# Seven-product pairs of a hybrid layer's attention: one wide matmul for both parts of the input, in place of two

## Chip, cores and metric

The kernel runs on one core of one Trainium2 chip. The metric is the device time of one execution in microseconds; the time before is the median of three runs. Beside the times there is one profiled execution with a trace of every instruction, and all durations and positions come from it. The core's engines are TensorE (PE in the profile; its weight loads are PEld), VectorE (DVE), ScalarE (ACT), GpSimd (POOL) and SyncE (SP), which here issues the weight transfers.

## What is computed

One decoder layer in fp32, on 512 tokens of width 1024: a SwiGLU feed-forward, a mixer, and a second feed-forward, each with a norm before and after. The mixer has two branches from one input projection `u @ w_in`: dilated attention with 12 heads in 3 groups, and a gated recurrence. Cut to the part around the change:

```python
u = rms_norm(h, mix_norm_pre[l])
proj = u @ w_in[l]
q, k, v, xr, yr, gl = jnp.split(proj, splits, axis=-1)
...
for g, (window, dilation) in enumerate(DILATED_GROUPS):
    o_g, lse_g = dilated_group_attention(q[:, :, g], k[:, :, g], v[:, :, g], ...)
alpha = jax.nn.softmax(jnp.stack(lses, axis=0), axis=0)
attn = jnp.einsum('gbsh,gbshe->bshe', alpha, jnp.stack(outs, axis=0))
...
gates = jax.nn.sigmoid(gl).reshape(B, S, N_BRANCHES, D_MODEL)
merged = gates[:, :, 0] * attn_d + gates[:, :, 1] * rec_d
h = h + rms_norm(merged @ w_out[l], mix_norm_post[l])
```

## The kernel before

**Three matmuls for one.** An fp32 operand x is kept as two tiles of a reduced format: a high part xh (a rounding copy on ScalarE, L302) and a low part xl (x minus xh on VectorE, L303); `split` at L301 issues both. A product w x is then wh xh + wh xl + wl xh, three matmuls that add up in one PSUM bank. Weights come from HBM in the order of one fixed stream (`raw_of`, L234, issued on SyncE, four buffers) and are split the same way into tiles of 1024 (`w8`, four buffers) or 512 columns (`w4`, two).

**Seven products for eight.** For two neighbouring blocks of 128 output columns (a "pair": a query head and its key head, or two blocks of the gates), the 2x2 block product (halves of the depth, halves of the tokens) is done with seven products p1 to p7 in place of eight (a Strassen-like scheme). Each product is 4 blocks of the depth by 3 matmuls, 128 x 128 weights against 256 tokens, in `seventh` (L709 to L717: L715 is wh xh, L716 wh xl, L717 wl xh). `w_forms` (L671) makes the seven weight combinations of a pair: adds on VectorE (L678, L679, L680 and one more) and three splits of 1024 columns and one of 512. `forms_of` (L615) makes the seven combinations of the input once, in three steps (`early` with L654 to L656, `middle`, `late`).

**A pair** (`seven`, L748) runs p1, p2, p6, p5, p7, p4, p3 into three accumulators of 256 columns. Products that share an accumulator add up in it, so intermediate values are copied away on the way: four ScalarE copies of 128 x 256 to SBUF (L759), and four VectorE adds of a bank and a copy (L764) give the four quarters of the result. Banks come from two pools, five called `acc` and three called `aux`.

**The attention stage.** After the first feed-forward's last product, `Boundary.block` (L530) adds the residual and norms each of four token blocks, and `Boundary.turn` (L545) transposes it in two halves: four transposes into a bank, a ScalarE copy of 512 (L552, the high part), a VectorE subtract of 512 (L553, the low part), and a ScalarE copy to `facc` (L554). The high and low parts of the mixer's input, `um_t`, are two tiles of high and two of low values. Then:
- `values_first` (L1114) computes the first group's values, 512 columns of weights against 128 tokens (L1123 to L1125), and transposes the last two blocks between;
- `values_two` (L1136) computes the two other groups' values by seven products of 24 matmuls each (L1165 to L1167; 512 columns wide), its weights' combinations (`add`, L1151) made on the chip from four large transfers `vals<-in_w` and the stream;
- `qk(0)` (L1237) runs three pairs (queries and keys of head 0 in the three groups); then for each of four heads `attend` (L1258) computes scores, the softmax and the output, beside the next head's `qk`;
- eight gate blocks as four pairs with sigmoids (L1374), and the product with the attention's output weights.

**The order.** A tile scheduler places the instructions of all engines from the program's text and its priorities: weight loads and their combinations and splits are ahead by `AHEAD` = 100, what empties PSUM by `EVAC` = 200. Each engine then works through its list in that fixed order. Waits are semaphores that the scheduler sets where data or buffers require them.

Of the kernel before, what the change touches and what calls it, by code (L numbers as in the profile page):

```python
# [16 lines left out]
P = 128  # L17
# [166 lines left out]
def hybrid_layer(ctx: ExitStack, tc: tile.TileContext, xT: bass.AP, xN: bass.AP, wst: bass.AP,  # L184
# [337 lines left out]
    class Boundary:  # L522

        def __init__(self, f, grow, his, los, kept):
            self.f, self.grow, self.his, self.los, self.kept = f, grow, his, los, kept
            self.u = {}

        def block(self, b, sums):  # L530
# [14 lines left out]
        def turn(self, b):  # L545
            for i, u in enumerate(self.u.pop(b)):
                ps = aux_ps()
                for j in range(4):
                    PE.transpose(ps[:, j * P:(j + 1) * P], u[:, j * P:(j + 1) * P], ident)
                src = ps.rearrange("p (k t) -> p k t", k=4)  # L550
                hi, lo = (t[:, :, b * P:(b + 1) * P] for t in (self.his[i], self.los[i]))
                ACT.activation(hi, src, AF.Copy)  # L552
                DVE.tensor_sub(lo, src, hi.bitcast(F32))  # L553
# [13 lines left out]
    def x_forms(gname, r, pool):  # L567

        spool[0] = pool
        ha, hc = hs["t"]  # L570
        x00, x01, x10, x11 = ha[:, :, 0:HB], ha[:, :, HB:T], hc[:, :, 0:HB], hc[:, :, HB:T]
        t, d = {}, {}

        def form(name, src, tile_=None):
            v = tile_ if tile_ is not None else big([P, 2, 4, HB])
            t[name] = v[:, 0], v[:, 1]
# [35 lines left out]
    def tx_slot(pool, bufs=1):  # L612
        return pool.tile([P, 2, 4, HB], F32R, name="tx", tag="tx", bufs=bufs)

    def forms_of(x, his, los, pool, copied, rb=None):  # L615


        spool[0] = pool
        fx = facc.rearrange("p k t -> p (k t)").rearrange("p (b c) -> p b c", b=4)

        def quarter(i, j):
            return fx[:, 2 * j:2 * j + 2, i * T:i * T + T]

        two = []

        def slot():
            if not copied and not two:
                v = rb()
                two.extend(v[:, 4 * i:4 * i + 4, :].rearrange("p (s j) t -> p s j t", s=2) for i in range(2))
            if two:  # L630
                return two.pop(0)
            return tx_slot(pool).rearrange("p s k t -> p s (k t)").rearrange("p s (b c) -> p s b c", b=2)

        x01, x10, x11 = quarter(0, 1), quarter(1, 0), quarter(1, 1)
        t, d = {}, {}
        for name, i, j in (("p1", 0, 0), ("p2", 1, 0), ("p3", 1, 1)):
            t[name] = tuple(z[i][:, :, HALVES[j]] for z in (his, los))

        def copies():
            for name in ("p1", "p2", "p3"):  # L640
                v = big([P, 2, 4, HB])
                for i in range(2):
                    nc.gpsimd.dma_start(v[:, i], t[name][i])
                t[name] = v[:, 0], v[:, 1]

        def form(name, v, src):
            t[name] = tuple(v[:, i].rearrange("p b (k t) -> p k b t", k=4) for i in range(2))
            split(v[:, 0], v[:, 1], src)

        def early():  # L650
            if copied:
                copies()
            d[1], d[2] = (pool.tile([P, 2, T], F32, name="ts", tag="s", bufs=2) for _ in range(2))
            DVE.tensor_sub(d[1], quarter(0, 0), x01)  # L654
            DVE.scalar_tensor_tensor(d[2], x11, -1.0, d[1], op0=ALU.mult, op1=ALU.subtract)
            DVE.tensor_sub(x01, x11, x01)  # L656

        def middle():
            form("p6", slot(), d[2])
            DVE.scalar_tensor_tensor(d[2], d[2], -1.0, x10, op0=ALU.mult, op1=ALU.subtract)  # L660
            form("p5", big([P, 2, 2, T]), d[1])

        def late():
            form("p7", big([P, 2, 2, T]), x01)
            form("p4", big([P, 2, 2, T]) if copied else slot(), d[2])

        return t, [early, middle, late]
# [39 lines left out]
                    "p6": b[:, :, lo], "p3": b[:, :, hi], "p4": d}  # L707

    def seventh(t, w, p, ps, start):  # L709
        if len(t[p][0].shape) == 4:  # L710
            ps = ps.rearrange("q (b t) -> q b t", b=2)
        for k in range(4):
            ks = slice(k * P, (k + 1) * P)
            wh, wl, xh, xl = w[p][:, 0, ks], w[p][:, 1, ks], t[p][0][:, k], t[p][1][:, k]
            PE.matmul(ps, wh, xh, start=start and k == 0, stop=False, skip_group_check=True)  # L715
            PE.matmul(ps, wh, xl, start=False, stop=False, skip_group_check=True)  # L716
            PE.matmul(ps, wl, xh, start=False, stop=k == 3, skip_group_check=True)  # L717
# [27 lines left out]
        seventh(t, w, "p4", v, False)  # L745
        u0(v)

    def seven(t, w, z, g, u, seen=lambda ap: ap):  # L748


        b, y = acc_ps()[:, :HB], acc_ps()[:, :HB]
# [9 lines left out]

        def sum_of(dst, ps, c):
            with tc.high_priority(offset=EVAC):
                DVE.tensor_add(dst, seen(ps), seen(c))  # L764

        product("p1", b, True)
        c1 = copy(b)
# [305 lines left out]
    for b in range(4):  # L1073
        nc.gpsimd.dma_start(hb(b), xN[b])
    grow1, grow2 = gains(ap1, 0, 1)
    um_t = [big([P, 4, T]) for _ in range(4)]
    um = act_of(um_t[:2], um_t[2:])
    kept_m = dpool.tile([4, P, D], F32, name="kept_m")
    bd1 = Boundary(0.5, grow2, um_t[:2], um_t[2:], kept_m)

    def block1(b, sums):
        bd1.block(b, sums)
# [14 lines left out]
    with ExitStack() as mx:  # L1097
# [38 lines left out]
        def values_two(steps, then):  # L1136
# [23 lines left out]
            def prod(p, w, pss, start):  # L1160
                for j, ps in enumerate(pss):
                    for k in range(4):
                        xh, xl = (x[:, k, j * P:j * P + P] if len(x.shape) == 3 else x[:, k, j, :] for x in t[p])
                        wh, wl = (w[k // 2][:, i, k % 2 * T:k % 2 * T + T] for i in range(2))
                        PE.matmul(ps, xh, wh, start=start and k == 0, stop=False, skip_group_check=True)  # L1165
                        PE.matmul(ps, xh, wl, start=False, stop=False, skip_group_check=True)
                        PE.matmul(ps, xl, wh, start=False, stop=k == 3, skip_group_check=True)  # L1167
# [46 lines left out]
            prod("p4", w4_, v, False)  # L1214
            copies([vals[2][:, j, :] for j in range(2)], v, -1.0)

        t, steps = forms_of(um, um_t[:2], um_t[2:], apool, False, rec_half)
# [19 lines left out]
        def qk(hd):  # L1237

            q, k = [], []
            for g in range(NG):  # L1240
                w = pair_of(("pair",) + pairs[hd][g])
                tq, tk = (apool.tile([P, T], F32, name="qk", tag="qk", bufs=QKB) for _ in range(2))
                if g == 0:
                    seven(t, w, acc_ps()[:, :HB], *([nat(x)[:, 2 * i:2 * i + 2] for i in range(2)] for x in (tq, tk)),
                          seen=lambda ap: ap.rearrange("q (p b r) -> q p b r", p=2, b=4))
# [142 lines left out]
    with ExitStack() as mx:  # L1388
# [202 lines left out]
        for c in range(KC):  # L1591
            if c < 3:
                ps = pss[c]
            else:
# [14 lines left out]
    bd2 = Boundary(1.0, grow4, his, los, kept)  # L1609
# [6 lines left out]
    end2 = ffn(2, u2, None, forms_of(u2, his, los, ap2, True), ap2, pss)  # L1616
    new_h()
    for b in range(4):
        nc.gpsimd.dma_start(hb(b), kept[b])
# [139 lines left out]
```

## Time and profile before

| | |
|---|---|
| median of three runs | 1215.32 us (1214.71 to 1215.39) |
| profiled execution, first to last instruction | 1213.2 us |
| median less that span | 2.1 us |
| mean granted TensorE clock | 0.999 |
| TensorE's instructions | 7754 matmuls, 7754 weight loads |
| VectorE, ScalarE | 1536 and 1393 instructions |
| HBM read, written | 138.06 MB, 6.29 MB |
| stage around the change | values from 369 us, a head's period 39.5 us, gates after the last head |

How to read the rows shown below. In a row of a group stand the line, the engine, the operation, output and inputs by their names in the program, the shape (partitions x elements), the count after "x", then the busy time in us and the mean duration of one in ns, and last the idle time of the engine just before them with what ended it. A row of the timeline begins with the start in us and the duration. A row of waits reads: engine, tile and line that waited, what it waited for, then the time in us in all, how often, and the longest. TensorE's matmuls overlap in the pipe: a duration there is longer than the distance to the next start.

### The profile page before, as it was taken

How to read it: one execution, taken by the hardware profiler on the slowest of the kernel's cores; microseconds unless marked ns; L12 is line 12 of the kernel's file. 1: busy time of each engine (PE TensorE's matmuls, PEld its weight loads, DVE VectorE, ACT ScalarE, POOL GpSimd, SP SyncE). 2: the span in 40 equal slices, each digit the busy share in tenths (PEclk: the TensorE clock that was granted, in tenths of full speed). 3: DMA queues.
4: the chain of work that ended last, by engine and by line, in shares of the span. 5: the costliest groups of instructions: out<-in, count | busy, mean ns of one | idle time of the engine just before them, and what ended most of it. 6: DMA issues, size and time to landing. Idle time of an engine off the chain costs nothing.

```text
span 1213.2 us, 19767 instructions
## 1 busy us (share of the span) xinstructions
PE 1203.3 (99%) x7754; PEld 1099.5 (91%) x7754; DVE 1010.1 (83%) x1536; ACT 815.9 (67%) x1393; POOL 26.1 (2%) x51
## 2 busy tenths in 40 slices
PE   9999999999999999999999999999999999999997
PEld 8899999999888999999989888888899999999996
DVE  7999888989689888888767899875799888889964
ACT  6566787887566565566735898844566677878763
POOL 0000000000011000000000000000100000000000
PEclk9999999999999999999999999999999999999999
DMA  7233333334624232222213342235443333433341
GB/s 266 87 102 125 123 139 111 135 120 155 245 109 143 83 100 96 71 96 87 91 67 123 130 148 88 90 119 179 152 140 110 120 136 107 137 115 129 123 173 70
DMA packets 45822, 149.83 MB, mean 124 GB/s; under 512 B 5152, under 2 KB 8608, under 8 KB 45728
## 3 DMA queue, kind: packets, MB, share of 16 engines
q1 hardware_dynamic: 38160, 131.09, 31.9%
q0 software_dynamic: 7280, 17.30, 4.3%
q8 instruction: 61, 1.00, 0.3%
q14 instruction: 33, 0.27, 0.1%
q10 hardware_dynamic: 288, 0.17, 0.0%
HBM read 138.06 MB, written 6.29 MB: 119 GB/s over the span
## 4 chain that ended last, share of the span: by engine, by line
PE 91%; DVE 5%; DMA 2%; ACT 1%; issue 1%; DVEq 0%
PE acc L715 14%; PE acc L716 14%; PE acc L717 14%; PE acc L315 7%; PE acc L317 7%; PE acc L316 7%; PE aux L966 4%; PE aux L967 3%; PE aux L968 3%; DVE w L303 2%; PE acc L433 2%; PE acc L431 2%; PE acc L432 2%; DMA raw<-in_w 2%; PE aux L433 1%; PE aux L431 1%
## 5 line engine op out<-in xcount | busy, mean ns | idle before, releaser
L717 PE MATMUL acc<-big,w 128*128 128x256 f32 x1240 | 351.8, 284 | 0.0
L715 PE MATMUL acc<-big,w 128*128 128x256 f32 x1240 | 351.6, 284 | 0.0
L716 PE MATMUL acc<-big,w 128*128 128x256 f32 x1240 | 351.3, 283 | 0.0
L303 DVE TENSOR_TENSOR w<-raw,w 128x1024 fp32r<-128x1024 f32 (+1 forms) x272 | 298.2, 1100 | 48.1 <-ACT w L302 41.3
L302 ACT ACTIVATE w<-raw 128x1024 fp32r<-128x1024 f32 (+1 forms) x272 | 259.7, 958 | 100.1 <-PE acc L317 44.9
L715 PEld LDWEIGHTS acc<-big,w 128*128 128x128 f32 x1240 | 237.6, 192 | 2.0
L716 PEld LDWEIGHTS acc<-big,w 128*128 128x128 f32 x1240 | 237.6, 192 | 1.7
L717 PEld LDWEIGHTS acc<-big,w 128*128 128x128 f32 x1240 | 237.7, 192 | 0.0
L966 PE MATMUL aux<-w,xf 128*128 128x512 f32 x224 | 87.5, 393 | 0.8 <-ACT w L302 0.7
L967 PE MATMUL aux<-w,xf 128*128 128x512 f32 x224 | 87.5, 391 | 0.0
L968 PE MATMUL aux<-w,xf 128*128 128x512 f32 x224 | 87.2, 389 | 0.0
L303 DVE TENSOR_TENSOR w<-s,w 128x1024 fp32r<-128x1024 f32 x51 | 62.4, 1223 | 3.7 <-ACT w L302 3.5
L302 ACT ACTIVATE w<-s 128x1024 fp32r<-128x1024 f32 x51 | 54.0, 1058 | 12.6 <-PE acc L717 9.2
L315 PE MATMUL acc<-xf,w 128*128 128x512 f32 (+1 forms) x168 | 59.1, 354 | 0.0
L316 PE MATMUL acc<-xf,w 128*128 128x512 f32 (+1 forms) x168 | 58.6, 350 | 0.0
L317 PE MATMUL acc<-xf,w 128*128 128x512 f32 (+1 forms) x168 | 58.5, 349 | 0.0
L729 ACT ACTIVATE c<-acc 128x256 f32<-128x256 f32 x74 | 28.2, 383 | 41.8 <-PE acc L717 41.8
L966 PEld LDWEIGHTS aux<-w,xf 128*128 128x128 f32 x224 | 41.9, 188 | 9.6 <-ACT w L302 1.3
L968 PEld LDWEIGHTS aux<-w,xf 128*128 128x128 f32 x224 | 42.1, 188 | 8.8
L315 PE MATMUL acc<-big,w 128*128 128x512 f32 x128 | 49.8, 389 | 0.0
L316 PE MATMUL acc<-big,w 128*128 128x512 f32 x128 | 49.8, 389 | 0.0
L317 PE MATMUL acc<-big,w 128*128 128x512 f32 x128 | 49.8, 389 | 0.0
(436 smaller groups left out, 2745.7 us busy)
## 6 DMA issues: line engine op xcount, KB each, us to landing
raw<-in_w SPq DMA_DIRECT2D x232, 512.0 KB, 3.5
big<-xf POOLq DMA_DIRECT2D x6, 512.0 KB, 3.9
gains<-in_rows POOLq DMA_DIRECT2D x5, 512.0 KB, 5.8
h<-in_x SPq DMA_DIRECT2D x8, 256.0 KB, 5.1
h<-in_xn POOLq DMA_DIRECT2D x4, 512.0 KB, 6.2
kept_m<-h POOLq DMA_DIRECT2D x4, 512.0 KB, 2.9
vals<-in_w SPq DMA_DIRECT2D x4, 512.0 KB, 5.9
h<-kept_m POOLq DMA_DIRECT2D x4, 512.0 KB, 5.4
```

Source lines behind the costliest of these rows:

```text
L302: state["split"] = ACT.activation(dh, src, AF.Copy).ins
L303: DVE.tensor_sub(dl, src, dh.bitcast(F32))
L315: PE.matmul(ps, wh, xh, start=first, stop=False)
L316: PE.matmul(ps, wh, xl, start=False, stop=False)
L317: PE.matmul(ps, wl, xh, start=False, stop=last)
L431: PE.matmul(ps, x.hi[k][:, bl], wh, start=k == 0 and not seeded, stop=False, skip_group_check=True)
L715: PE.matmul(ps, wh, xh, start=start and k == 0, stop=False, skip_group_check=True)
L716: PE.matmul(ps, wh, xl, start=False, stop=False, skip_group_check=True)
L717: PE.matmul(ps, wl, xh, start=False, stop=k == 3, skip_group_check=True)
L966: PE.matmul(ps, xh, wh, start=first and j == 0, stop=False, skip_group_check=True)
L967: PE.matmul(ps, xh, wl, start=False, stop=False, skip_group_check=True)
L968: PE.matmul(ps, xl, wh, start=False, stop=j == 1, skip_group_check=True)
```

## The change

The 16 pairs of the attention stage (12 of queries and keys, 4 of gates) run in a new function, `seven_wide`. The high weights multiply both parts of the input in one matmul of 512 columns, [xh | xl], into the two halves of one bank; the low weights times xh are added into the upper half. The two halves of a bank are added when a result leaves it. The products run in the order p1, p5, p6, p2, p7, p3, p4 with four accumulators; a partial sum that two results share is moved from bank to bank by ScalarE (`move`). So that one operand can span both parts, the mixer's input lies in four tiles, each with the high and low part of two depth blocks, and a `turn` splits each transposed half in two steps. The feed-forwards' pairs keep the old form. The core of the diff:

```diff
-                src = ps.rearrange("p (k t) -> p k t", k=4)
-                hi, lo = (t[:, :, b * P:(b + 1) * P] for t in (self.his[i], self.los[i]))
-                ACT.activation(hi, src, AF.Copy)
-                DVE.tensor_sub(lo, src, hi.bitcast(F32))
+                for ks, *two in self.parts(i):
+                    src = ps.rearrange("p (k t) -> p k t", k=4)[:, ks]
+                    hi, lo = (t[:, :, b * P:(b + 1) * P] for t in two)
+                    ACT.activation(hi, src, AF.Copy)
+                    DVE.tensor_sub(lo, src, hi.bitcast(F32))
...
-    um_t = [big([P, 4, T]) for _ in range(4)]
+    um_t = [big([P, 2, 2, T]) for _ in range(4)]
...
+    def seven_wide(t, w, g, u, seen=lambda ap: ap):
+        b, v, z, y = (acc_ps() for _ in range(4))
+        def two(ps):
+            return ps[:, :HB], ps[:, HB:]
+        def product(p, ps, start):
+            at = t[p].at
+            part, cross = ps.rearrange("q (s c) -> q s c", s=2), two(ps)[1]
...
+            for k in range(4):
+                ks = slice(k * P, (k + 1) * P)
+                wh, wl = w[p][:, 0, ks], w[p][:, 1, ks]
+                PE.matmul(part, wh, at(BOTH, k), start=start and k == 0, stop=False, skip_group_check=True)
+                PE.matmul(cross, wl, at(0, k), start=False, stop=k == 3, skip_group_check=True)
+        def move(dst, src):
+            with tc.high_priority(offset=EVAC):
+                ACT.activation(dst, src, AF.Copy)
+        def fold(ps, dst=None):
+            out = tpool.tile([P, HB], F32, name="c", tag="c", bufs=CB) if dst is None else dst
+            x, y_ = two(ps) if dst is None else map(seen, two(ps))
+            with tc.high_priority(offset=EVAC):
+                ACT.activation(out, x, AF.Copy)
+                DVE.tensor_add(out, y_, out)
+            return out
+        def sum_of(dst, ps, c):
+            x, y_ = two(ps)
+            with tc.high_priority(offset=EVAC):
+                DVE.tensor_add(c, x, c)
+                DVE.tensor_add(dst, seen(y_), seen(c))
+        product("p1", b, True)
+        move(y, b)
+        product("p5", z, True)
+        c5 = fold(z)
+        product("p6", y, False)
+        move(v, y)
+        c6 = fold(y)
+        product("p2", b, False)
+        fold(b, g[0])
+        product("p7", v, False)
+        move(b, v)
+        sum_of(u[1], v, c5)
+        product("p3", z, False)
+        sum_of(g[1], z, c6)
+        product("p4", b, False)
+        fold(b, u[0])
...
-                    seven(t, w, acc_ps()[:, :HB], *([x[:, h] for h in HALVES] for x in (tq, tk)))
+                    seven_wide(t, w, *([x[:, h] for h in HALVES] for x in (tq, tk)))
...
-            seven(t, pair_of(("pair", 52 + c, 53 + c)), acc_ps()[:, :HB], [g[:, h] for h in HALVES],
-                  [u[:, h] for h in HALVES])
+            seven_wide(t, pair_of(("pair", 52 + c, 53 + c)), [g[:, h] for h in HALVES], [u[:, h] for h in HALVES])
```

The rest of the diff passes the new layout through (`Form.at(s, k)` gives block k of part s, high or low or both). In the program as scheduled, the order of instructions differs from before only between the end of the first feed-forward's last product and the product with the attention's output weights.

More of the change, by code (lines that the diff above doesn't have):

```diff
@@ L522, in hybrid_layer, with __init__ @@
     class Boundary:
-        def __init__(self, f, grow, his, los, kept):
-            self.f, self.grow, self.his, self.los, self.kept = f, grow, his, los, kept
+        def __init__(self, f, grow, parts, kept):
+            self.f, self.grow, self.parts, self.kept = f, grow, parts, kept
             self.u = {}
@@ L549, in turn, with __init__, form_of @@
                     PE.transpose(ps[:, j * P:(j + 1) * P], u[:, j * P:(j + 1) * P], ident)
-                src = ps.rearrange("p (k t) -> p k t", k=4)
-                hi, lo = (t[:, :, b * P:(b + 1) * P] for t in (self.his[i], self.los[i]))
-                ACT.activation(hi, src, AF.Copy)
-                DVE.tensor_sub(lo, src, hi.bitcast(F32))
-                ACT.activation(fb(b, FHALVES[i]), ps, AF.Copy)
+                for ks, *two in self.parts(i):
[3 more added lines that the diff above has]
+                    DVE.tensor_sub(lo, src, hi.bitcast(F32))
+                ACT.activation(fb(b, FHALVES[i]), ps, AF.Copy)
+    class Form:
+        def __init__(self, at):
+            self.at = at
+    BOTH = slice(0, 2)
+    def form_of(v):
+        return Form(lambda s, k: v[:, s, k])
     def act_of(his, los):
@@ L575, in form @@
             v = tile_ if tile_ is not None else big([P, 2, 4, HB])
-            t[name] = v[:, 0], v[:, 1]
+            t[name] = form_of(v)
             split(v[:, 0], v[:, 1], src)
@@ L613, in tx_slot, with forms_of @@
         return pool.tile([P, 2, 4, HB], F32R, name="tx", tag="tx", bufs=bufs)
-    def forms_of(x, his, los, pool, copied, rb=None):
+    def forms_of(at, pool, copied, rb=None):
         spool[0] = pool
@@ L636, in forms_of @@
         for name, i, j in (("p1", 0, 0), ("p2", 1, 0), ("p3", 1, 1)):
-            t[name] = tuple(z[i][:, :, HALVES[j]] for z in (his, los))
+            t[name] = at(i, j)
         def copies():
@@ L643, in copies @@
                     nc.gpsimd.dma_start(v[:, i], t[name][i])
-                t[name] = v[:, 0], v[:, 1]
+                t[name] = form_of(v)
         def form(name, v, src):
-            t[name] = tuple(v[:, i].rearrange("p b (k t) -> p k b t", k=4) for i in range(2))
+            five = v.rearrange("p s b (k t) -> p s b k t", k=4)
+            t[name] = Form(lambda s, k: five[:, s, :, k])
             split(v[:, 0], v[:, 1], src)
@@ L709, in seventh @@
     def seventh(t, w, p, ps, start):
-        if len(t[p][0].shape) == 4:
+        at = t[p].at
+        if len(at(0, 0).shape) == 3:
             ps = ps.rearrange("q (b t) -> q b t", b=2)
@@ L713, in seventh @@
             ks = slice(k * P, (k + 1) * P)
-            wh, wl, xh, xl = w[p][:, 0, ks], w[p][:, 1, ks], t[p][0][:, k], t[p][1][:, k]
+            wh, wl, xh, xl = w[p][:, 0, ks], w[p][:, 1, ks], at(0, k), at(1, k)
             PE.matmul(ps, wh, xh, start=start and k == 0, stop=False, skip_group_check=True)
@@ L746, in seven_on, with seven @@
         u0(v)
-    def seven(t, w, z, g, u, seen=lambda ap: ap):
+    def seven_wide(t, w, g, u, seen=lambda ap: ap):
[3 more added lines that the diff above has]
+        def product(p, ps, start):
+            at = t[p].at
+            part, cross = ps.rearrange("q (s c) -> q s c", s=2), two(ps)[1]
+            if len(at(0, 0).shape) == 3:
+                part = ps.rearrange("q (s b t) -> q s b t", s=2, b=2)
+                cross = cross.rearrange("q (b t) -> q b t", b=2)
+            for k in range(4):
[34 more added lines that the diff above has]
+        fold(b, u[0])
+    def seven(t, w, z, g, u):
         b, y = acc_ps()[:, :HB], acc_ps()[:, :HB]
@@ L763, in sum_of @@
             with tc.high_priority(offset=EVAC):
-                DVE.tensor_add(dst, seen(ps), seen(c))
+                DVE.tensor_add(dst, ps, c)
         product("p1", b, True)
@@ L1075, in hybrid_layer @@
     grow1, grow2 = gains(ap1, 0, 1)
-    um_t = [big([P, 4, T]) for _ in range(4)]
-    um = act_of(um_t[:2], um_t[2:])
+    um_t = [big([P, 2, 2, T]) for _ in range(4)]
+    um = Act(*([um_t[k // 2][:, s, k % 2, :] for k in range(KC)] for s in range(2)))
     kept_m = dpool.tile([4, P, D], F32, name="kept_m")
-    bd1 = Boundary(0.5, grow2, um_t[:2], um_t[2:], kept_m)
+    bd1 = Boundary(0.5, grow2, lambda i: [(slice(2 * j, 2 * j + 2), um_t[2 * i + j][:, 0], um_t[2 * i + j][:, 1])
+                                          for j in range(2)], kept_m)
     def block1(b, sums):
@@ L1162, in prod @@
                     for k in range(4):
-                        xh, xl = (x[:, k, j * P:j * P + P] if len(x.shape) == 3 else x[:, k, j, :] for x in t[p])
+                        xh, xl = (x[:, j, :] if len(x.shape) == 3 else x[:, j * P:j * P + P]
+                                  for x in (t[p].at(0, k), t[p].at(1, k)))
                         wh, wl = (w[k // 2][:, i, k % 2 * T:k % 2 * T + T] for i in range(2))
@@ L1215, in values_two @@
             copies([vals[2][:, j, :] for j in range(2)], v, -1.0)
-        t, steps = forms_of(um, um_t[:2], um_t[2:], apool, False, rec_half)
+        t, steps = forms_of(lambda i, j: Form(lambda s, k: um_t[2 * i + k // 2][:, s, k % 2, HALVES[j]]),
+                            apool, False, rec_half)
         values_first()
@@ L1243, in qk @@
                 if g == 0:
-                    seven(t, w, acc_ps()[:, :HB], *([nat(x)[:, 2 * i:2 * i + 2] for i in range(2)] for x in (tq, tk)),
-                          seen=lambda ap: ap.rearrange("q (p b r) -> q p b r", p=2, b=4))
+                    seven_wide(t, w, *([nat(x)[:, 2 * i:2 * i + 2] for i in range(2)] for x in (tq, tk)),
+                               seen=lambda ap: ap.rearrange("q (p b r) -> q p b r", p=2, b=4))
                 else:
-                    seven(t, w, acc_ps()[:, :HB], *([x[:, h] for h in HALVES] for x in (tq, tk)))
+                    seven_wide(t, w, *([x[:, h] for h in HALVES] for x in (tq, tk)))
                 q.append(tq)
@@ L1608, in hybrid_layer @@
     grow3, grow4 = gains(ap2, 2, 3)
-    bd2 = Boundary(1.0, grow4, his, los, kept)
+    bd2 = Boundary(1.0, grow4, lambda i: [(slice(0, 4), his[i], los[i])], kept)
     slots = [spare(ap2)[i] for i in ("e", "tt", "tx")] + [w8]
@@ L1615, in hybrid_layer @@
                      {3: [lambda: bd2.turn(2)], 4: [lambda: bd2.turn(3)]})
-    end2 = ffn(2, u2, None, forms_of(u2, his, los, ap2, True), ap2, pss)
+    end2 = ffn(2, u2, None, forms_of(lambda i, j: [z[i][:, :, HALVES[j]] for z in (his, los)], ap2, True), ap2, pss)
     new_h()
```

## The prediction

> **What bounds the kernel now.** I read the page from the top: the busy time of each engine, the chain of work that ended last, then the costliest groups.
>
> ```profile
> span 1213.2 us, 19767 instructions
> PE 1203.3 (99%) x7754; PEld 1099.5 (91%) x7754; DVE 1010.1 (83%) x1536; ACT 815.9 (67%) x1393; POOL 26.1 (2%) x51
> ...
> PE 91%; DVE 5%; DMA 2%; ACT 1%; issue 1%; DVEq 0%
> ...
> L717 PE MATMUL acc<-big,w 128*128 128x256 f32 x1240 | 351.8, 284 | 0.0
> L715 PE MATMUL acc<-big,w 128*128 128x256 f32 x1240 | 351.6, 284 | 0.0
> L716 PE MATMUL acc<-big,w 128*128 128x256 f32 x1240 | 351.3, 283 | 0.0
> ```
>
> TensorE is busy 1203.3 of 1213.2 us and carries 91% of the chain. The view of waits, for TensorE over the whole span, says the same from the other side:
>
> ```profile
> PE aux L315 <- ACT w L302: 1.5, 1, 1.5
> PE aux L1043 <- DVE eps L228: 1.1, 1, 1.1
> PE aux L966 <- ACT w L302: 0.7, 3, 0.2
> PE aux L549 <- DVE u L541: 0.2, 1, 0.2
> ```
>
> These 3.5 us are all, and none of them lies in the attention stage. So there the time is the number of matmuls times their spacing, as long as no new wait appears. A matmul's own duration (284 ns) overlaps its neighbours, so I take spacings from start to start in the timeline, once at a width of 256 and once of 512:
>
> ```profile
> 436.18 0.28 PE L715 MATMUL acc<-big,w 128*128 128x256 f32 x1
> ...
> 437.50 0.28 PE L717 MATMUL acc<-big,w 128*128 128x256 f32 x1
> ```
>
> ```profile
> 367.72 0.39 PE L1123 MATMUL acc<-w,big 128*128 128x512 f32 x1
> ...
> 369.08 0.39 PE L1165 MATMUL aux<-w,big 128*128 128x512 f32 x1
> 369.31 0.40 PE L1166 MATMUL aux<-w,big 128*128 128x512 f32 x1
> ```
>
> Eleven matmuls lie between the first two rows: 1.32/11 = 120 ns. Six lie between 367.72 and 369.08: 1.36/6 = 226.7 ns. Twice 120 is 240, so a 512-wide matmul saves 13.3 ns on two 256-wide ones. The reader is to see how small this is: doubling the width takes the spacing up by 106.7 ns, so some 13.3 ns are a fixed part of each matmul.
>
> The other engines decide whether that saving arrives. The table of stretches, by stage (columns: window, length, busy time and instructions of PE, PEld, DVE, ACT, POOL, then the clock, the DMA share and GB/s):
>
> ```profile
> 360.50:400.50 40.00, 40.00 (x177) 32.80 (x176) 39.72 (x39) 26.04 (x34) 7.33 (x15) 1.00 0.45 137
> 476.80:516.30 39.50, 39.49 (x328) 38.98 (x327) 33.09 (x67) 23.33 (x55) 0.00 (x0) 1.00 0.26 87
> 478.00:501.50 23.50, 23.49 (x193) 23.04 (x193) 22.89 (x53) 15.89 (x44) 0.00 (x0) 1.00 0.31 98
> ```
>
> Row one is the seven products of the values, row two one whole head (its attention and the next head's three pairs), row three the denser part of that head. VectorE is full in the first (39.72 of 40.00), nearly full in the third (22.89 of 23.50), and has 6.4 us to spare in the second.
>
> **The change, part by part.**
>
> *Matmuls.* 16 pairs (12 of queries and keys, 4 of gates) x 7 products x 4 blocks of k = 448 steps, each with two 256-wide matmuls replaced by one 512-wide: 448 x 13.3 ns = **-6.0 us**. The third stays. No row shows a moving operand made of two separate runs of 256; bounds are 0 (it runs as two) and 6.0, and I take 6.0, since the write fills one bank as the quoted 512-wide ones do. The Trainium skill ("TensorE: Matmul & The Clock Gate", section "Back-to-back issue gap") gives an isolated gap of N/2.4 + 2.5 ns, so 109 and 216 ns: an estimate by that page saves 2.5 ns a step, 1.1 us in all. The trace's 120 and 226.7 disagree with it by 11 ns at each width, and the measurement decides.
>
> *More evacuation.* Per pair ScalarE goes from four 256-wide copies to four of those plus three 512-wide moves from bank to bank; VectorE from four 256-wide adds to eight. The groups by shape, the one line that moves 512 columns within PSUM, and two adds in the timeline:
>
> ```profile
> L759 ACT ACTIVATE c<-acc 128x256 f32<-128x256 f32 x72 | 27.2, 379 | 27.4 <-PE acc L717 26.2
> L764 DVE TENSOR_TENSOR qk<-acc,c 128x256 f32<-128x256 f32 x36 | 15.1, 419 | 4.1 <-PE acc L717 4.1
> L303 DVE TENSOR_TENSOR w<-raw,w 128x1024 fp32r<-128x1024 f32 x210 | 255.8, 1222 | 40.8 <-ACT w L302 33.9 <-PE acc L717 5.6
> L302 ACT ACTIVATE w<-raw 128x1024 fp32r<-128x1024 f32 x210 | 221.2, 1056 | 64.2 <-PE acc L317 44.9 <-PE acc L717 9.0 <-PE acc L1167 3.2
> ```
>
> ```profile
> L1172 ACT ACTIVATE acc<-aux x4: 582/582/582, 372.0 to 396.7; 128x512 f32<-128x512 f32 x4
> ```
>
> ```profile
> 475.61 0.42 DVE L764 TENSOR_TENSOR qk<-c 128x256 f32<-128x256 f32 x1
> 475.94 0.42 DVE L764 TENSOR_TENSOR qk<-acc,c 128x256 f32<-128x256 f32 x1
> ```
>
> A head has three pairs. ScalarE gains at most 9 x 0.582 = 5.2 us: 23.3 + 5.2 = 28.5 of 38.3, not a bound. VectorE gains 12 adds at 0.33 us apart: 33.1 + 4.0 = 37.1. TensorE's own period falls by 84 steps x 13.3 ns = 1.1, from 39.45 to 38.3. So VectorE still fits, by 1.2 us, if its idle time can be used. The waits of VectorE in that head:
>
> ```profile
> DVE w L303 <- ACT w L302: 2.8, 5, 0.7
> DVE s L678 <- DMA raw<-in_w: 1.5, 1, 1.5
> DVE s L679 <- DMA raw<-in_w: 1.4, 1, 1.4
> DVE qk L764 <- PE acc L717: 1.0, 1, 1.0
> ```
>
> The waits for ScalarE and TensorE can be filled by the new adds; the 2.9 us for weights (1.5 + 1.4) come from transfers and may stay. I take it that they shrink, because the adds run ahead of the weight forms and the forms then arrive later at transfers already landed.
>
> *New waits in a pair.* A product now adds into a bank that a ScalarE move must first fill. Between the move's source and the product that needs it lies one other product, 4 x (226.7 + 120) = 1.39 us. A bare move, counted from the start of its product's last matmul, takes 0.28 + 0.58 = 0.86 and is hidden. Behind a weight split of 1.056 us that has just begun it takes 1.92, and TensorE waits 0.5. What is queued behind such a move on ScalarE are exponentials and the next splits; TensorE's p6, p7 or p4 waits for it. p4's move also waits for VectorE's add of p2, which can stand behind a 1.22 us split. Bounds: 0, and 48 moves x 0.53 = 25 us if each met a fresh split. I followed the two queues in the order of the changed program through one head with these durations: most moves meet a free engine, and the head's statistics, which go over VectorE and a small matmul and now stand behind the added adds, come about 0.3 us late. That leaves 0.4 us a head, 4 x 0.4 = **+1.6**, and about 0.15 at p4 in some four or five of the other pairs, **+0.7**. These two are estimates near the lower bound.
>
> *The input's layout.* High and low halves of the mixer's input now lie together in four tiles, so each block's transposed half is split in two 256-wide steps in place of one 512-wide: eight more operations on each of ScalarE and VectorE. Only the last block's are late for anything: VectorE's next work is the values' stage, quoted here from the timeline of before:
>
> ```profile
> 360.54 1.29 DVE L553 TENSOR_TENSOR big<-aux,big 128x512 fp32r<-128x512 f32 x2 [1.64 <-ACT big L552]
> 361.89 1.22 DVE L654 TENSOR_TENSOR ts<-facc 128x1024 f32<-128x1024 f32 x1
> 363.23 1.23 DVE L655 SCALAR_TENSOR_TENSOR ts<-facc,ts 128x1024 f32<-128x1024 f32 x1
> 364.37 1.22 DVE L656 TENSOR_TENSOR facc<-facc 128x1024 f32<-128x1024 f32 x1
> 365.50 1.22 DVE L303 TENSOR_TENSOR big<-ts,big 128x1024 fp32r<-128x1024 f32 x1
> 366.75 1.23 DVE L1151 TENSOR_TENSOR vals<-vals 128x1024 f32<-128x1024 f32 x1
> 367.90 4.62 DVE L303 TENSOR_TENSOR w<-raw,w 128x1024 fp32r<-128x1024 f32 x4
> ```
>
> Two splits took 1.29; four at 0.33 apart take 1.41, and ScalarE's four feed them one by one. I put L654 0.13 to 0.6 later, at 362.25 (+0.36).
>
> *Order in the values' stage.* The scheduler changes it, and this stage has no slack on VectorE: L1166 started at 369.31, 0.19 us after its weights' low part (367.90 + 1.22 = 369.12). VectorE's steps here lie 1.14 apart (363.23 to 364.37). In the changed program the sum of weights (L1151) moves up to fourth, ahead of the split of a form. It needs the third of four transfers:
>
> ```profile
> vals<-in_w SPq DMA_DIRECT2D x4, 512.0 KB, 5.9
> ```
>
> In before that add started 0.11 us behind its turn (365.50 + 1.14 = 366.64, against 366.75), which may have been that transfer. At the fourth place its turn comes at 362.25 + 0.2 (the gap behind L654) + 3 x 1.14 = 365.87; so VectorE waits 0 to 0.9 us. And TensorE goes on to p6 after p1, p2 and six matmuls: 369.08 + 48 x 0.2267 + 6 x 0.2267 = 381.3; the low half of p6's weights is VectorE's 18th step after L654's place: 362.25 + 0.2 + 17 x 1.14 + 1.22 = 383.1, or 384.0 with the transfer's wait. In before that operand's step has the same number, but TensorE ran all of p5 (24 matmuls) first, and came to p6 only at 385.4. Loss 1.8 to 2.7 us; I take **+2.6**, near the end with the wait, because of those 0.11 us. p5's form, split later now, is ready at 362.25 + 0.2 + 0.9 + 21 x 1.14 + 1.22 = 388.5, and TensorE, done with p6 at 384.0 + 22 x 0.2267 = 389.0, doesn't wait again. Everything behind it shifts by the same.
>
> **Sum** against the profiled execution: -6.0 + 1.6 + 0.7 + 2.6 = -1.1, span 1213.2 to 1212.1. The median of the runs lies 2.1 us above that span (1215.32), so 1214.2; I say **1214.3**.
>
> **Rivals.**
>
> *A, the covers hold.* If the values' stage costs nothing (the transfer lands in time, VectorE is ahead) the 2.6 go: 1211.7. For it: TensorE waits nowhere in this stage before. Against it: VectorE is busy 39.72 of 40.00 there. Chance 0.22.
>
> *B, VectorE sets the pace in the heads* (slower). If the 2.9 us of waits for weights stay beside the added adds, a head takes 37.1 + 2.9 = 40.0 in place of my 38.3 + 0.4 = 38.7: 4 x 1.3 = +5.2, 1219.5. It decides as soon as more than 38.7 - 37.1 = 1.6 us of idle time can't be used. For it: 22.89 of 23.50 in the dense part. Against it: 3.8 us of VectorE's waits there (2.8 + 1.0) are for other engines, and new adds can fill them. Chance 0.20.
>
> *C, the wide matmul saves nothing*, running as two: 1214.3 + 6.0 = 1220.3. Against it: the fixed part of 13.3 ns shows at both widths. Chance 0.08. A saving of 1.1 us, the Trainium skill's by the page named above, would give 1219.2 and is counted here.
>
> **How the numbers follow.** Forecast 0.50, A 0.22, B 0.20, C 0.08. The forecast's own range is 1212.0 to 1217.5 (losses from 2.6 to 8.2 in place of 4.9). The whole range is 1211.0 to 1219.5: it takes in A, most of B, and leaves C and the far ends out. A measurement of this kernel tells about 0.2% (2.4 us) from no change: 1212.9 and 1217.7. Faster 0.26 (A but 0.03, and 0.07 of the forecast), slower 0.26 (B but 0.05, C, and 0.03 of the forecast), same 0.48.
>
> **What would show it.** Matmuls of 512 followed by 256: 346.7 ns a step, not 360. TensorE's waits: up to 2.6 us at the values' p1 and p6 for VectorE's weights, some tenths per head behind moves and adds. Head period 38.7 and VectorE busy about 37 of it. Wrong would be: a head of 39.5 or more (B), no wait in the values' stage (A), a step of 360 (C), or TensorE waiting over 0.2 us for a move in most pairs.

## The result and the profile after

The changed kernel takes 1217.49 us (median of 11 runs, 1217.02 to 1218.61), the kernel before 1215.32 beside it. The ratio is 1.0018, interval 1.001 to 1.0025: it is slower by about 2.2 us. I had forecast 1214.3 and a slight gain. The profiled execution has a span of 1215.4 us, 2.2 more than before (1213.2).

First the page of the changed kernel, engines and chain:

```profile
span 1215.4 us, 18988 instructions
PE 1200.5 (99%) x7306; PEld 1073.9 (88%) x7306; DVE 1030.6 (85%) x1608; ACT 835.9 (69%) x1449; POOL 26.2 (2%) x51
...
PE 89%; DVE 5%; ACT 3%; DMA 2%; issue 1%; SPq 0%; DVEq 0%; ACTq 0%
```

TensorE has 448 matmuls fewer and is still the bound, but ScalarE's share of the chain went from 1% to 3%. The view of TensorE's waits has new rows in it:

```profile
PE aux L1237 <- DVE w L303: 2.5, 2, 1.3
PE aux L315 <- ACT w L302: 1.5, 1, 1.5
PE acc L779 <- ACT acc L784: 1.4, 2, 1.1
PE aux L1112 <- DVE eps L228: 1.1, 1, 1.1
PE aux L1386 <- DVE xch L1383: 0.9, 1, 0.9
PE aux L1035 <- ACT w L302: 0.6, 3, 0.2
PE aux L549 <- DVE u L541: 0.2, 1, 0.2
```

L1237 is the values' product, L779 the wide matmul behind a move (L784), L1386 the small matmul of the softmax statistics (`exchange`). 4.8 us are new. The view misses waits of the weight load in front of a matmul; the view of line L784 has those too, in the columns "who waited for it (us, times)":

```profile
  PEld acc L779: 4.3, 8
  PE acc L779: 1.4, 2
```

These overlap in part with the matmul's own work, so I measure the loss another way: by the starts of the same matmuls in both timelines. Before (first product of the values; it was shown at 369.08), first pair, then the first matmul of the attention of heads 1, 2 and 3, and the last matmul of the attention's output:

```profile
407.39 0.28 PE L715 MATMUL acc<-big,w 128*128 128x256 f32 x1
...
477.16 0.27 PE L1268 MATMUL aux<-qk 128*128 128x128 f32 x1
...
516.62 0.27 PE L1268 MATMUL aux<-qk 128*128 128x128 f32 x1
...
556.08 0.27 PE L1268 MATMUL aux<-qk 128*128 128x128 f32 x1
...
627.18 0.39 PE L317 MATMUL acc<-attn,w 128*128 128x512 f32 x1
```

and after:

```profile
368.27 0.39 PE L1236 MATMUL aux<-w,big 128*128 128x512 f32 x1
...
409.42 0.39 PE L779 MATMUL acc<-big,w 128*128 128x512 f32 x1
...
479.77 0.27 PE L1340 MATMUL aux<-qk 128*128 128x128 f32 x1
...
518.29 0.27 PE L1340 MATMUL aux<-qk 128*128 128x128 f32 x1
...
556.89 0.27 PE L1340 MATMUL aux<-qk 128*128 128x128 f32 x1
...
629.14 0.39 PE L317 MATMUL acc<-attn,w 128*128 128x512 f32 x1
```

| part (us) | before | after | difference | forecast |
|---|---|---|---|---|
| values, p1 to the first pair | 38.31 | 41.15 | +2.84 | +2.6 |
| first pairs and head 0 | 69.77 | 70.35 | +0.58 | -1.5 |
| head 1 | 39.46 | 38.52 | -0.94 | -0.7 |
| head 2 | 39.46 | 38.60 | -0.86 | -0.7 |
| last head, gates, output | 71.10 | 72.25 | +1.15 | -0.7 |
| stage | 258.10 | 260.87 | +2.77 | -1.1 |

(The forecast's column splits its sum: 28 steps a pair, 0.4 a head, the 0.7 of the other pairs shared between the second and the last row.) So three rows came out as forecast, and two lost about 2 us each. Each experiment below was judged by its time and by this **stage** (values' p1 to the attention's output), since the feed-forwards outside it differ from run to run: the changed program reached the values 0.8 us earlier in its profiled run than before did, with the same matmuls, and the waits of L1035 in the second feed-forward, for splits of weights, add up to 0.6 us there and to 2.5 in another run. The stage itself repeats well: the one program that ran as two experiments (e7 and e11) has 253.46 and 253.51.

### The profile page after: what moved, and what is told of

Same layout as the page of the kernel before. It is cut to its first block, busy times and chain, and to the rows that moved or that the text cites. A ratio compares the mean times of both kernels' runs of the same rounds, so it can differ in the third digit from the quotient of the medians.

```text
span 1215.4 us, 18988 instructions
## 1 busy us (share of the span) xinstructions
PE 1200.5 (99%) x7306; PEld 1073.9 (88%) x7306; DVE 1030.6 (85%) x1608; ACT 835.9 (69%) x1449; POOL 26.2 (2%) x51
## 4 chain that ended last, share of the span: by engine, by line
PE 89%; DVE 5%; ACT 3%; DMA 2%; issue 1%; SPq 0%; DVEq 0%; ACTq 0%
PE acc L729 10%; PE acc L731 10%; PE acc L730 10%; PE acc L315 7%; PE acc L317 7%; PE acc L316 7%; PE acc L779 7%; PE aux L1035 4%; PE aux L1036 4%; PE aux L1037 4%; PE acc L780 3%; DVE w L303 2%; PE acc L433 2%; PE acc L432 2%; PE acc L431 2%; DMA raw<-in_w 1%
## 5 line engine op out<-in xcount | busy, mean ns | idle before, releaser
L729 PE MATMUL acc<-big,w 128*128 128x256 f32 x920 | 260.4, 283 | 0.0
L731 PE MATMUL acc<-big,w 128*128 128x256 f32 x920 | 260.3, 283 | 0.0
L730 PE MATMUL acc<-big,w 128*128 128x256 f32 x920 | 260.3, 283 | 0.0
L729 PEld LDWEIGHTS acc<-big,w 128*128 128x128 f32 x920 | 176.2, 192 | 1.9
L730 PEld LDWEIGHTS acc<-big,w 128*128 128x128 f32 x920 | 176.3, 192 | 1.7
L731 PEld LDWEIGHTS acc<-big,w 128*128 128x128 f32 x920 | 176.3, 192 | 0.0
L779 PE MATMUL acc<-big,w 128*128 128x512 f32 x320 | 115.2, 398 | 0.3 <-ACT acc L784 0.3
L780 PE MATMUL acc<-big,w 128*128 128x256 f32 x320 | 90.6, 283 | 0.0
L1035 PE MATMUL aux<-w,xf 128*128 128x512 f32 x224 | 87.5, 393 | 0.6 <-ACT w L302 0.6
L779 PEld LDWEIGHTS acc<-big,w 128*128 128x128 f32 x320 | 60.1, 188 | 13.7 <-ACT acc L784 0.6
L780 PEld LDWEIGHTS acc<-big,w 128*128 128x128 f32 x320 | 60.5, 189 | 0.1
L1035 PEld LDWEIGHTS aux<-w,xf 128*128 128x128 f32 x224 | 41.9, 188 | 9.3 <-ACT w L302 1.2
```

The costliest lines, as they stand in the source:

```text
L779: PE.matmul(part, wh, at(BOTH, k), start=start and k == 0, stop=False, skip_group_check=True)
L780: PE.matmul(cross, wl, at(0, k), start=False, stop=k == 3, skip_group_check=True)
L1035: PE.matmul(ps, xh, wh, start=first and j == 0, stop=False, skip_group_check=True)
```

## The experiments

My theory after the result: the saving is there, and four things eat it. The layout reorders the values' stage; p4's move stands behind VectorE's add of p2; head 0's statistics wait; and in the gates a move stands behind a table load on ScalarE. The rival: ScalarE and VectorE carry too much altogether, so TensorE's spacing no longer sets the time.

| run | time | ratio to before (95%) | stage | against before |
|---|---|---|---|---|
| changed kernel | 1217.49 | 1.0018 (1.001 to 1.0025) | 260.87 | +2.77 |
| e1 layout only, old pairs | 1217.43 | 1.0016 (1.0007 to 1.0025) | 260.90 | +2.80 |
| e2 narrow matmuls | 1221.77 | 1.0054 (1.004 to 1.0068) | 265.21 | +7.11 |
| e3 hold | 1217.82 | 1.0019 (1.0011 to 1.0028) | 259.24 | +1.14 |
| e4 fresh bank | 1214.71 | 0.9997 (0.9988 to 1.0006) | 258.23 | +0.13 |
| e5 hold and fresh bank | 1214.08 | 0.9987 (0.9978 to 0.9995) | 256.23 | -1.87 |
| e6 late exponential | 1216.28 | 1.0002 (0.9993 to 1.0011) | 258.93 | +0.83 |
| e7 all three | 1211.06 | 0.9959 (0.9946 to 0.9973) | 253.46 | -4.64 |
| e8 all three, narrow | 1217.02 | 1.0013 (1.0004 to 1.0022) | 260.37 | +2.27 |
| e9 old pairs, repaired | 1215.78 | 1.0005 (0.9997 to 1.0014) | 258.52 | +0.42 |
| e10 before, late exponential | 1215.18 | 0.9999 (0.999 to 1.0008) | 257.97 | -0.13 |
| e11 all three, again | 1211.91 | 0.997 (0.9958 to 0.9981) | 253.51 | -4.59 |

**e1: the layout alone.**

```diff
-                    seven_wide(t, w, *([x[:, h] for h in HALVES] for x in (tq, tk)))
+                    seven(t, w, acc_ps()[:, :HB], *([x[:, h] for h in HALVES] for x in (tq, tk)))
```

(and the same in the two other places)

> Only the input's new layout (high and low parts in one tile, each transposed half split in two steps), with the old pairs of three narrow matmuls and the old order of products. My theory: the loss of 2.8 us in the values' stage comes from the layout alone, because VectorE's list there is already the changed one: TensorE waits 1.3 us for the first weights of p1 and 1.5 us for those of p6, and nothing else changes. So 1215.3 + 2.8 = about 1218.1, heads at 39.5 us a period. Rival: the loss belongs to the wide pairs' load on VectorE and ScalarE, and the layout alone costs nothing: 1215.3.

Measured: 1217.43, stage +2.80. The stage is the theory's number; the time lies 0.7 us below the 1218.1 expected. Its waits in the stage are the two of the values, and no other:

```profile
PE aux L1237 <- DVE w L303: 2.4, 2, 1.3
```

The changed kernel is no slower than this one: its pairs bring as much as they lose. Where the layout's loss comes from shows in VectorE's timeline of the changed kernel, against the one that the prediction shows of before:

```profile
363.95 1.22 DVE L669 TENSOR_TENSOR facc<-facc 128x1024 f32<-128x1024 f32 x1
366.27 1.23 DVE L1221 TENSOR_TENSOR vals<-vals 128x1024 f32<-128x1024 f32 x1 [1.10 <-DMA vals<-in_w]
367.41 1.22 DVE L303 TENSOR_TENSOR rb<-ts,rb 128x1024 fp32r<-128x1024 f32 x1
368.55 4.62 DVE L303 TENSOR_TENSOR w<-raw,w 128x1024 fp32r<-128x1024 f32 x4
```

The sum of weights (L1221) stands fourth, waits 1.10 us for its transfer, and holds back p1's weights (368.55 in place of 367.90). TensorE's timeline shows both waits:

```profile
368.27 0.39 PE L1236 MATMUL aux<-w,big 128*128 128x512 f32 x1
369.82 0.50 PE L1237 MATMUL aux<-w,big 128*128 128x512 f32 x1 [1.16 <-DVE w L303]
370.16 0.40 PE L1238 MATMUL aux<-w,big 128*128 128x512 f32 x1
...
381.51 0.61 PE L1236 MATMUL aux<-w,rb 128*128 128x512 f32 x2
383.44 0.50 PE L1237 MATMUL aux<-w,rb 128*128 128x512 f32 x1 [1.32 <-DVE w L303]
383.78 0.39 PE L1238 MATMUL aux<-w,rb 128*128 128x512 f32 x1
```

A wait costs more than its bracket says: the matmul that waited starts late, and the next follows after 0.34 us (369.82 to 370.16) where 0.227 is usual.

**e2: is the saving there?**

```diff
-                PE.matmul(part, wh, at(BOTH, k), start=start and k == 0, stop=False, skip_group_check=True)
+                for s in range(2):
+                    PE.matmul(part[:, s], wh, at(s, k), start=start and k == 0 and s == 0, stop=False, ...)
```

> The changed kernel, but the 512-wide matmul of each step is issued as two of 256, one for each half of the bank; everything else as changed. My theory: TensorE sets the pace except at some ten waits, so taking the saving back costs 448 x 12.5 ns = 5.6 us, less some 0.5 us because each product now covers the moves by 0.05 us more: 1217.5 + 5.1 = about 1222.6. Rival: VectorE or ScalarE set the pace, so the spacing of the matmuls hardly matters: 1217.5 to 1219.

Measured: 1221.77, 4.3 us above the changed kernel, and 4.3 by the stage. TensorE sets the pace. Over the steps of the changed kernel the median distances are 232 ns behind the wide and 117 ns behind the narrow matmul, 349 a step in place of 360 (347 in e7 below, with fewer waits): 11 to 13 ns, or 4.9 to 5.8 us in 448 steps. The expectation went by 12.5 ns and 5.6 us; 1.3 of them are missing here, most of them in the first pairs and head 0, which lose 1.0 us (71.32 against 70.35) where 168 steps of 12.5 ns make 2.1: the wait of 0.9 us for the softmax statistics is not in this run. The heads show the saving plainest: 39.63 us against 38.52, 13.2 ns a step. In the changed kernel a clean stretch of the timeline gives the spacing:

```profile
494.84 0.39 PE L779 MATMUL acc<-big,w 128*128 128x512 f32 x1
...
496.57 0.39 PE L779 MATMUL acc<-rb,w 128*128 128x512 f32 x1
```

Five steps in 1.73 us: 346 ns each, against 360 before.

**e3: hold the weight sum.**

```diff
-            w1, w2 = form(g0), form(g1)
+            w1 = form(g0)
+            tail = state["low"]
+            w2 = form(g1)
             steps[0]()
-            add(sd, u0, u1)
+            with tc.issue_after(tail):
+                add(sd, u0, u1)
```

(`state["low"]` is VectorE's last subtract in `split`)

> The changed kernel, with one hold on VectorE's order: the first sum of the values' weights, which needs the third of four transfers, is issued after the split of p1's weights. By that p5's input form is split before it, and TensorE runs p1, p2, p5, p6 in full again. My theory: both waits of the values' stage (1.3 and 1.5 us) go: 1217.5 - 2.8 = about 1214.7. Rival: VectorE is full in that stage, so the waits only move to a later product: 1216.5 to 1217.5.

Measured: 1217.82. A miss. Both waits of TensorE in the values' stage are gone and the first pair starts 38.52 us after p1 (41.15 in the changed kernel), but p4 of that first pair now waits. TensorE, ScalarE and VectorE there:

```profile
416.02 0.28 PE L780 MATMUL acc<-big,w 128*128 128x256 f32 x1
417.34 0.50 PE L779 MATMUL acc<-rb,w 128*128 128x512 f32 x1 [1.04 <-ACT acc L784]
```

```profile
416.70 0.58 ACT L784 ACTIVATE acc<-acc 128x512 f32<-128x512 f32 x1 [1.56 <-DVE qk L791]
```

```profile
412.91 0.69 DVE L692 TENSOR_TENSOR s<-s,raw 128x512 f32<-128x512 f32 x1 [1.06 <-DMA raw<-in_w]
...
415.06 1.22 DVE L303 TENSOR_TENSOR w<-s,w 128x1024 fp32r<-128x1024 f32 x1
416.19 0.41 DVE L791 TENSOR_TENSOR qk<-acc,qk 128x256 f32<-128x256 f32 x1
```

Read from the top: p4 waits for the move, the move for VectorE's add of p2 (L791, the last reader of the bank that the move overwrites), that add for its turn behind a split, and the whole list for a weight transfer. In the changed kernel the values' delay hid that transfer. So the stage gains 1.63 us on the changed kernel, but the time doesn't: outside the stage the profiled span is 956.4 us, against 954.6 in the changed kernel. In the second feed-forward this run's profile has a wait of 1.6 us (L1035), near waits of VectorE of 1.8 and 0.7 us for weight transfers. Whether such waits also make the 11 times lie so high (1215.74 to 1219.31) isn't shown.

**e4: a bank of its own for p4.**

```diff
-        b, v, z, y = (acc_ps() for _ in range(4))
+        b, v, z, y, r = (acc_ps() for _ in range(5))
...
-        move(b, v)
+        move(r, v)
...
-        product("p4", b, False)
-        fold(b, u[0])
+        product("p4", r, False)
+        fold(r, u[0])
```

> The changed kernel, with a fifth accumulator in a pair: the partial sum for p4 is moved into a bank of its own, and no longer into the bank of p2, which VectorE must first have read. My theory: the waits of p4 for that move, seven times 0.2 to 0.35 us with the slower matmul behind each, some 2 us in all, go, and those for the table load and the transfer on ScalarE stay: about 1215.6. Rival: with five banks a pair, the next pair waits for its banks instead: 1217.5 or more.

Measured: 1214.71, 2.8 us less (1.9 were expected). First pairs and head 0 fall from 70.35 to 68.00 us: p4's waits are gone, and head 0's statistics, which wait 0.9 us in the changed kernel, no longer stop TensorE. The second is not the bank's doing alone: the scheduler also placed the statistics' first small matmul later, behind 115 steps of the pairs where it stood behind 98. In the changed kernel's timeline p4 is late by 0.9 us in all in this part, and the statistics by 0.9; the rest of the 2.35 isn't assigned, and no run separates the two. The gates' loss stays, as expected.

**e5: hold and fresh bank.**

> The hold on VectorE's first weight sum (as in the run e3) and the fifth accumulator (as in e4) together. In e3 the values' stage ended 2.6 us earlier, but p4 of the first pair then waited 1.2 us for a move that stood behind VectorE's add of p2, and that add behind a sum of weights whose transfer had not landed. My theory: with a bank of its own p4's move doesn't need that add, so both gains come in full: 1214.7 (e4) - 2.6 = about 1212.1. Rival: the transfers land at a fixed time, so the start of the pairs can't move up and the time stays at e4's 1214.7.

Measured: 1214.08, 2.0 above the 1212.1 expected; the stage falls by 2.0 us below e4's and not by 2.6. The rival's number (1214.7) is nearer, but not its cause, since the pairs do start earlier. The values give all (38.56 us in place of 41.30), but head 0 takes 68.85 in place of 68.00: its first scores now wait 0.7 us for a result's last add. The median falls by 0.6 only: outside the stage the profiled span is 955.7 us, against 954.6 in e4. Why it is longer there isn't shown.

**e6: the late exponential.**

```diff
-            ACT.activation(facc[:, c + 1, :], u, AF.Sigmoid, scale=-1.0)
+            gate_last = ACT.activation(facc[:, c + 1, :], u, AF.Sigmoid, scale=-1.0).ins
...
-        ACT.activation(ex, ex, AF.Exp)
+        with tc.issue_after(gate_last):
+            ACT.activation(ex, ex, AF.Exp)
```

> The changed kernel, with the recurrence's first exponential held on ScalarE until the gates' last sigmoid is issued. In the changed kernel that exponential stands between the gates' sigmoids, so the table is loaded again (1.28 us) ahead of a sigmoid (0.63 us), both ahead of the move that p6 of a gate pair waits for 1.1 us. My theory: that wait goes, with the slower matmul behind it: 1217.5 - 1.3 = about 1216.2. Rival: the sigmoid alone or a split takes the table's place ahead of the move: 1217 to 1217.5.

Measured: 1216.28; the last part falls from 72.25 to 70.34 us, and the view shows no wait of TensorE there. What it removes, in the changed kernel, ScalarE and TensorE:

```profile
593.41 1.28 ACT L1486 ACT_TABLE_LOAD   x1
...
595.99 1.05 ACT L302 ACTIVATE w<-raw 128x1024 fp32r<-128x1024 f32 x1
597.05 1.28 ACT L1449 ACT_TABLE_LOAD   x1
598.35 0.63 ACT L1449 ACTIVATE facc<-g 128x512 f32<-128x512 f32 x1
598.88 0.58 ACT L784 ACTIVATE acc<-acc 128x512 f32<-128x512 f32 x1
```

```profile
598.15 0.28 PE L780 MATMUL acc<-big,w 128*128 128x256 f32 x1
599.51 0.51 PE L779 MATMUL acc<-rb,w 128*128 128x512 f32 x1 [1.08 <-ACT acc L784]
```

An exponential of the recurrence, scheduled among the gates' sigmoids, costs a table load to go (L1486) and one to come back (L1449). The move behind the second makes p6 1.24 us late. In the same pair p7 is late by another 0.48 us, for a move behind a split that waited 1.48 us for a transfer; that wait goes with e6 too, and whether the loads had brought it about isn't shown. The kernel before has the same two loads, at 591.40 and 595.37, and TensorE waits for neither:

```profile
595.37 1.28 ACT L1379 ACT_TABLE_LOAD   x1
```

The load row agrees with the Trainium skill ("ScalarE: Activation LUTs", section "What ACT_TABLE_LOAD costs": 1283 ns). The same section adds about 1380 ns of drain; here the load begins within 0.02 us of the end of the split before it (595.99 + 1.05), and no run here shows the drain.

**e7, e11: all three; e8: with narrow matmuls.**

> All three repairs: the hold on VectorE's weight sum, the fifth accumulator, the late exponential. My theory: they add, since they lie in three stages: 1212.1 - 1.3 = about 1210.8, that is 4.4 us under the kernel before; what is left of the saving of 5.6 is some 1 us of waits. Rival: what one frees is given back at the next transfer (as in e3): 1212 to 1214.

> All three repairs, but with the 512-wide matmul of each step issued as two of 256. My theory: with hardly any waits left the saving shows almost in full, so this is 448 x 12.5 ns = 5.6 us (at least 5) above the run with the three repairs, near 1216.2. Rival: the wide matmul's saving is smaller than the spacing says (in e2 it was 4.3 us): 1214.5 to 1215.2.

> The three repairs once more (as e7), beside the two runs above, for the interval. My theory: 1211 within 0.7 us, so 0.35% under the kernel before. Rival: the 1211.06 of e7 was a lucky sample of five, since the waits for transfers in the feed-forwards move by a microsecond and more from run to run: 1212.5 to 1214.

Measured: 1211.06 and again 1211.91 (0.2 beyond the band named), stage -4.64 and -4.59; e8 1217.02. The repairs add, and the result takes 0.3 to 0.4% less than the kernel before and about 0.5% less than the changed one. e8 lies 6.0 us above e7, and its stage 6.9: 1.2 of these are a wait of its own (a matmul in the attention, for ScalarE's copy of a transposed block), which leaves 5.7 for the spacing, 12.7 ns a step. What is left of TensorE's waits in e7:

```profile
PE aux L1035 <- ACT w L302: 2.5, 3, 1.6
PE aux L315 <- ACT w L302: 1.5, 1, 1.5
PE aux L1112 <- DVE eps L228: 1.1, 1, 1.1
PE aux L1343 <- DVE qk L791: 0.6, 1, 0.6
PE aux L549 <- DVE u L541: 0.2, 1, 0.2
```

Only L1343 lies in the stage. L1035 is in the second feed-forward, 0.6 us in the changed kernel's run and 2.5 here, with the same instructions there. The profiled executions of e6, e7 and e11, where these waits add up to 1.8 us and more, are the slowest of their runs (1212.48 in e7, with a median of 1211.06), so such waits can account for the spread of some 2 us; for the other runs that isn't shown.

**e9, e10: are the repairs worth something without the wide pairs?** e9 is e1 with the hold and the late exponential, e10 the kernel before with the late exponential alone (in both behind the two sigmoids of the last pair, where e6 names the second).

> The old pairs of three narrow matmuls, with the new layout, the hold on VectorE's weight sum and the late exponential. My theory: the layout cost its 2.8 us only by the order in the values' stage; with the hold that is gone, and the exponential was hidden in the old pairs. So the stage from the last product before it to the attention's output is within 0.3 us of the kernel before, about 1215.3, and the 4.3 us of the run with three repairs are the wide matmul's own. Rival: the repairs themselves are worth 2 us or more in the old pairs too: 1213 or less.

> The kernel before, with only the late exponential. My theory: one table load fewer on ScalarE, but TensorE waits for no ScalarE copy in the gates there, so nothing: 1215.3. Rival: the exponential cost something in the old gates too: 1214 or less.

Measured: 1215.78 (stage +0.42, a little above the 0.3 expected) and 1215.18. No: in the old pairs a table load stops nobody, and the hold only takes the layout's loss back. The gain of e7 is that of the wide matmuls: 5.06 us of stage between e9 and e7.

## Why the prediction was wrong

**Right.** The matmul saving (forecast 13.3 ns a step and 6.0 in all; measured 11 ns by the changed kernel's median step and 13 to 14 in its clean stretches, 4.9 to 6.3; in the stage, 5.06 with the repairs). The values' stage, by its very steps (forecast +2.6, measured +2.84): fourth place of the sum, the transfer's wait of up to 0.9 (measured 1.10), p6 ahead of its weights; e1 shows that the layout alone does it. The heads' period (38.7 against 38.52 and 38.60): VectorE is busy 36.47 of 38.52 us and doesn't set the pace, as the row shows:

```profile
479.77:518.29 38.52, 38.44 (x244) 34.21 (x242) 36.47 (x80) 26.75 (x63) 0.00 (x0) 1.00 0.27 90
```

So rival B, which would have been slower, is not what happened, nor is C.

**Wrong: the step "new waits in a pair", in its size and in the place.** I took 2.3 us for all moves and statistics, near the lower bound, from one head followed by hand; by the stage they cost about 6.2 (the 2.3, and the 3.9 of the two parts below). That head's number holds where I followed it. But the pairs outside are others: in the first pairs and head 0 the moves behind VectorE's add of p2 and the late statistics cost 2.1 us more than forecast (e4 brings that part back to -1.8 us, against -1.5 forecast), and in the gates 1.85 more, where I had looked at splits and exponentials as what stands ahead of a move and not at a table load (e6 brings that part to -0.76, against -0.7). The two parts together miss by 3.9 us, which is the whole distance between -1.1 and +2.77. Two of the chains, p4's and the statistics', were named, so there the kind of wait was right and its price was not; the load of a table was not named at all. I had put head 0's statistics, like every head's, 0.3 us late; they hold TensorE up for 0.9. I had put p4's chain over VectorE at 0.15 us in four or five pairs; the timeline of the changed kernel has it in six, 0.16 to 0.24 us at p4's first matmul and 0.10 more at the one behind it. Here p4 of the second pair starts 0.34 us after the matmul before it, where 0.117 is usual:

```profile
428.29 0.28 PE L780 MATMUL acc<-big,w 128*128 128x256 f32 x1
428.63 0.50 PE L779 MATMUL acc<-rb,w 128*128 128x512 f32 x1
```

In the two profiled executions the rest of the span is 0.5 us shorter with the change (954.6 against 955.1), which makes 2.2 of the stage's 2.77. What stays open is how far that holds for the other executions: over all the runs here the rest lies between 954.0 and 958.2 us.

## What to carry to other kernels

In this kernel a copy to SBUF that only empties a bank could come late; a move that the next product adds onto can't, and everything ahead of it on its engine, on the engine that frees its target, and in that engine's transfers becomes TensorE's wait. Give such a move a target that nobody else must release, and look for table loads ahead of it. And price a part that repeats in each place where its neighbours differ, not in one.

## What the hardware showed that I had not expected

- After each wait of TensorE shown here, the matmul behind the late one is late too: 0.34 us at a width of 512 in place of 0.227 (369.82 to 370.16, 383.44 to 383.78), 0.10 to 0.11 us a wait on top of it.
- Where ScalarE goes from sigmoids to an exponential and back, a load of 1.28 us stands each time (593.41, 597.05); copies in between need none (48 moves, and no load right ahead of any).
- A change of layout without any change of arithmetic cost 2.8 us, because a transfer's landing and the place of one add in VectorE's list met (e1).
